# Two-layer decoder trunk on one core: other tiles for the turned first features, and another spacing of the first slabs

## The chip, the core and the metric

The kernel runs on one core of a Trainium2 chip. A core has a matmul engine (TensorE, PE in the profile; its weight loads are shown as PEld), VectorE (DVE), ScalarE (ACT), GpSimd (POOL) and SyncE (SP), which issues most of the transfers from memory. The engines run side by side, each through its own list of instructions, and wait for one another by semaphores. The metric is the time of one execution on the device in microseconds (us). The time before is the median of 3 runs.

## The reference

What is computed, cut to the part that the change touches, is a trunk of two layers over 256 tokens of width 2048. Each layer has a mixing part (pooling and memory attention in the first, differential and memory attention in the second) and a feed-forward part:

```
D_MODEL, SEQ, D_FF = 2048, 256, 8192

def squared_relu_mlp(h, w1, w2):
    z = jax.nn.relu(h @ w1)
    return (z * z) @ w2

for i in range(2):
    ...
    x = x + jnp.concatenate([token_out, mem_out], axis=-1) @ w_out[i]
    x = x + squared_relu_mlp(rms_norm(x, ffn_norm[i]), w_ff1[i], w_ff2[i])
```

All weights and activations are 32-bit floats. The change touches the feed-forward part alone, and so acts twice, once in each layer.

## The kernel before

**Precision.** Each weight and each activation is split into a high half (a rounded copy, made on ACT at L187) and a low half (what is left, made on DVE at L190). A product takes high by high, low by high and high by low. The halves of the weights stand in two rings of 6 slots, hi_ring and lo_ring; the class Feed loads the weights (DMAs from SP at L151 to L155, into buffers named raw, slab and room, and accumulating DMAs from POOL at L162) and splits them up to 3 jobs ahead of PE.

**Features and tiles.** The 8192 hidden features are 64 columns of 128, numbered by when they are made. The first 8 come out of first_jobs: a product with fewer multiplications (seven where eight would be plain, in the manner of Strassen) over the first 1024 columns of w_ff1, in seven accumulators p0 to p6 that hold seven banks of PSUM. The other 56 come out of up_tile, one at a time, tiles 0 to 55. A tile is 16 blocks of 128 x 128 weights; a block is one matmul of 512 columns (L448) and one of 256 (L450). All tiles from 2 on accumulate in the one PSUM bank left, named x_bank. After a tile, ACT copies the bank out (evict, L809), and only then can PE start in it again. Some steps later the feature is squared and split into z, and for each pair of features the four sums that the cheap product needs are made (combine, into sit).

**Slabs.** The second product, z by w_ff2, uses the cheap scheme as well for half of the rows and columns that it covers. It is cut into slabs; a slab is a pair of features by 1024 columns, four jobs (0 to 3) with two, one, two and two products of three matmuls each (product, L922, L924, L925; 21 matmuls of 512 columns in all). The seven accumulators serve two halves g = 0 and 1 of the output columns in turn; between them, swap copies the partial sums out and in again (L1080, L1072). The eight slabs numbered -8 to -1 are those of first_jobs. When the last of them ends, close_first puts the seven accumulators together (copies on ACT, adds on DVE, L1011).

**The turn.** The results of first_jobs stand with tokens on the partitions, and z wants features there. So turn_first, called four times (h = 0 to 3), transposes two features each on PE (L1044) through x_bank, evicts them (L809) and puts them through the same squaring (L1048, L1053) and splitting (L820, L824) as the tiles. The tuple turned_at names the tiles ahead of which this happens. It also sets the numbering: the list feat gives each turned pair the next two numbers, so that the tiles behind it get numbers higher by two, and slabs take the features by their numbers.

**The order of the work.** tiles_at(p) says at which tile the slab p is to begin. From it a list of jobs is made, each with a due time in tiles: job 0 of slab p+1, jobs 1 and 2 of slab p and job 3 of slab p-1 share a place. While the tiles are written out, due(u) runs all jobs that are due, at every fourth block of a tile, and at least two jobs ahead of a tile and one behind a turn if they are ready. A job isn't ready while its accumulators belong to the other half, or while the features (z) or the sums (sit) of its slab aren't made. A job that isn't ready holds up all jobs behind it. Twelve jobs are left for the end, between the tiles of the last product. The framework's scheduler may then shift instructions on an engine, within what data and buffers allow.

```
        turned_at = (18, 26, 34, 42)
...
        for u in range(2, 56):
            due(u, 2)
            if u in turned_at:
                turn_first(turned_at.index(u))
                due(u, 1)
...
            up_tile(index[u], bank(), inner(u))
```

Of the kernel before, what the change touches and what calls it, by code (L numbers as in the profile page):

```python
# [303 lines left out]
def program(ctx, tc, plan, dry, xT, memT, par, lam, cst, wst, yT):  # L304
# [468 lines left out]
    def ffn(l, xs, tags, done, z, sums_in, f_place):  # L773
# [20 lines left out]
        z_done, sit_done, summed_up = set(), set(), set()  # L794
        z_free = {j: j < 8 for j in range(NK)}
        sit_free = [False] * 4
        turned_at = (18, 26, 34, 42)
        feat, index = [], []
        for u in range(56):
            if u in turned_at:  # L800
# [378 lines left out]
        def tiles_at(p):  # L1179

            if p <= 0:
                return 9.08 + 0.86 * p
            return 9.08 + 0.78 * p if p <= 47 else 45.74 + 1.6 * (p - 47)

        jobs = []
        for p in range(-9, len(slabs) + 1):
            for j, s in enumerate((p + 1, p, p, p - 1)):
                if -8 <= s < len(slabs):
                    when_due = tiles_at(p) + j * (tiles_at(p + 1) - tiles_at(p)) / 4
                    jobs.append((when_due, s, j))  # L1190
# [321 lines left out]

    x_in = []
    down = ffn(0, fx, ("S1", "S0"), lambda n: resid_done(n, [(x_in[0], G_KV)], False), *made)
    x_kv = sp.tile([P, NK, 512], F32R, tag="S2", name="x_kv")
    x_in.append(x_kv)
# [237 lines left out]
    made = out_tiles(1, cat1, lead1, [15, 11], fx1, flush, (0, 1, 3, 7, 10), "S2")  # L1754

    down = ffn(1, fx1, ("S2", "S1"), lambda n: nc.sync.dma_start(yT[:, n, :], resid[:, n, :]), *made)
    down()
    flush()
# [82 lines left out]
```

## Time and profile before

| what | us |
|---|---|
| median of 3 runs | 2001.18 |
| lowest and highest of them | 1998.41, 2003.38 |
| the profiled execution | 2000.19 |
| its span, first to last instruction | 1998.4 |
| PE busy | 1989.0 |
| DVE busy | 1769.7 |
| ACT busy | 1547.3 |

The profiled execution is the one that all views show. Its span is 1.8 us shorter than its time. The feed-forward part of layer 0 stands roughly between 260 and 920 us of the span, that of layer 1 between 1330 and 1990 us. A row of a timeline gives the start in us, the length, the engine, the line, the operation with output and input, and in brackets the idle time before it and what ended it. Matmuls are pipelined: the length of one (0.39 us for 512 columns) is longer than the distance to the next start, and the distance is what counts for the time. In the windows, the numbers behind the stretch are its length, the busy time of PE, PEld, DVE, ACT and POOL with their instruction counts, the clock that was granted to TensorE (1.00 is full), the share of the DMA engines, and GB/s.

### The profile page before, as it was taken

Reading aid. Unit: us, or ns where it says so; the run is one execution under the profiler, and the core shown is the slowest. Engines: PE = TensorE matmul, PEld = TensorE weight load, DVE = VectorE, ACT = ScalarE, POOL = GpSimd, SP = SyncE. Lnnn points to the kernel's source line nnn. Section 1 sums busy time; section 2 is a strip of 40 time slices with the busy share of each in tenths; the row PEclk is TensorE's granted clock in tenths of the full one; section 3 lists DMA queues with packets and bytes.
Section 4 is the critical chain, followed back from the end, with each engine's and each line's share of the span. In section 5 each row is a group of like instructions: output and inputs, shape, how many; then the busy total and the mean of one; then the engine's idle time right before and its main releaser. Section 6 shows DMA issues by size and latency. Waiting matters only on the chain.

```text
span 1998.4 us, 31885 instructions
## 1 busy us (share of the span) xinstructions
PE 1989.0 (100%) x10386; PEld 1691.0 (85%) x10386; DVE 1769.7 (89%) x3252; ACT 1547.3 (77%) x2858; POOL 221.5 (11%) x261
## 2 busy tenths in 40 slices
PE   9999999999999999999999999999999999999999
PEld 7888888888888888888888889888888888888888
DVE  8888889999999999889765698989999999999988
ACT  7766677788888878778665699777778888878775
POOL 0000011111111211100000000001111112111110
PEclk9999999999999999999999999999999999999999
DMA  9556578988888888765565534568888888887775
GB/s 318 175 191 192 190 203 217 248 223 244 232 236 229 229 218 236 212 192 187 185 235 192 169 127 143 191 197 232 235 223 241 226 241 234 229 248 194 221 211 145
DMA packets 147623, 424.29 MB, mean 212 GB/s; under 512 B 16640, under 2 KB 19328, under 8 KB 147456
## 3 DMA queue, kind: packets, MB, share of 16 engines
q1 hardware_dynamic: 110448, 355.12, 53.0%
q0 software_dynamic: 36864, 67.13, 20.4%
q8 instruction: 81, 1.33, 0.3%
q14 instruction: 86, 0.70, 0.1%
q10 hardware_dynamic: 144, 0.01, 0.0%
HBM read 420.10 MB, written 2.10 MB: 211 GB/s over the span
## 4 chain that ended last, share of the span: by engine, by line
PE 98%; DMA 1%; DVE 0%; ACT 0%; issue 0%; SPq 0%; ACTq 0%
PE x_bank L448 22%; PE x_bank L450 11%; PE p L925 10%; PE p L922 10%; PE p L924 10%; PE wo L448 6%; PE wo L450 3%; PE u L448 2%; PE ff L448 1%; PE u L450 1%; PE q L482 1%; PE q L484 1%; PE k L482 1%; PE q L483 1%; PE v L482 1%; PE k L483 1%
## 5 line engine op out<-in xcount | busy, mean ns | idle before, releaser
L187 ACT CAST hi_ring<-raw 128x512 fp32r<-128x512 f32 x937 | 572.8, 620 | 229.0 <-DVE lo_ring L190 59.6
L190 DVE TENSOR_TENSOR lo_ring<-raw,hi_ring 128x512 fp32r<-128x512 f32 x937 | 633.6, 688 | 106.5 <-ACT hi_ring L187 92.4
L448 PE MATMUL x_bank<-fx,hi_ring 128*128 128x512 f32 x1728 | 542.4, 395 | 1.6 <-ACT room L809 1.6
L450 PEld LDWEIGHTS x_bank<-fx,lo_ring 128*128 128x128 f32 x1728 | 325.2, 188 | 74.7 <-DVE lo_ring L190 1.0
L190 DVE TENSOR_TENSOR lo_ring<-room,hi_ring 128x1024 fp32r<-128x1024 f32 x256 | 312.7, 1223 | 47.2 <-ACT hi_ring L187 44.5
L187 ACT CAST hi_ring<-room 128x1024 fp32r<-128x1024 f32 x256 | 268.8, 1053 | 97.0 <-PE x_bank L448 50.1
L450 PE MATMUL x_bank<-fx,lo_ring 128*128 128x256 f32 x1728 | 340.6, 279 | 0.1
L448 PEld LDWEIGHTS x_bank<-fx,hi_ring 128*128 128x128 f32 x1728 | 287.0, 189 | 28.8 <-ACT room L809 3.9
L190 DVE TENSOR_TENSOR lo_ring<-slab,hi_ring 128x1024 fp32r<-128x1024 f32 (+1 forms) x256 | 244.3, 954 | 28.2 <-ACT hi_ring L187 25.1
L187 ACT CAST hi_ring<-slab 128x1024 fp32r<-128x1024 f32 (+1 forms) x256 | 211.8, 835 | 50.0 <-PE p L924 23.1
L162 POOL DMA_DIRECT2D slab<-in_w x128 | 110.6, 864 | 1256.1 <-DVE lo_ring L190 1244.0
L922 PE MATMUL p<-hi_ring,sit 128*128 128x512 f32 x480 | 188.5, 393 | 0.0
L924 PE MATMUL p<-hi_ring,sit 128*128 128x512 f32 x480 | 187.5, 391 | 0.0
L925 PE MATMUL p<-lo_ring,sit 128*128 128x512 f32 x480 | 186.0, 390 | 0.0
L162 POOL DMA_DIRECT2D room<-in_w x128 | 110.5, 863 | 487.3 <-DVE lo_ring L190 421.9
L448 PE MATMUL wo<-cat,hi_ring 128*128 128x512 f32 x512 | 161.6, 397 | 0.0
L922 PE MATMUL p<-hi_ring,z 128*128 128x512 f32 x368 | 144.9, 394 | 0.0
L925 PE MATMUL p<-lo_ring,z 128*128 128x512 f32 x368 | 143.7, 391 | 0.3 <-DVE lo_ring L190 0.3
L924 PE MATMUL p<-hi_ring,z 128*128 128x512 f32 x368 | 143.9, 391 | 0.0
L450 PEld LDWEIGHTS wo<-cat,lo_ring 128*128 128x128 f32 x512 | 95.9, 188 | 22.3
L925 PEld LDWEIGHTS p<-lo_ring,sit 128*128 128x128 f32 x480 | 89.9, 188 | 20.6 <-DVE lo_ring L190 1.4
L922 PEld LDWEIGHTS p<-hi_ring,sit 128*128 128x128 f32 x480 | 90.0, 188 | 14.1 <-ACT p L1072 0.6
(415 smaller groups left out, 3522.1 us busy)
## 6 DMA issues: line engine op xcount, KB each, us to landing
raw<-in_w SPq DMA_DIRECT2D x466, 512.0 KB, 4.2
slab<-in_w SPq DMA_DIRECT2D x128, 512.0 KB, 5.7
room<-in_w SPq DMA_DIRECT2D x128, 256.0 KB, 4.7
slab<-in_w POOLq DMA_DIRECT2D x128, 256.0 KB, 5.1
room<-in_w POOLq DMA_DIRECT2D x128, 256.0 KB, 5.6
memraw<-in_mem SPq DMA_DIRECT2D x5, 512.0 KB, 3.6
resid<-in_x SPq DMA_DIRECT2D x8, 256.0 KB, 5.3
out_y<-resid SPq DMA_DIRECT2D x16, 128.0 KB, 1.9
```

The lines of the kernel that those rows point to most:

```text
L162: self.nc.gpsimd.dma_start(t, self.wst[h, :, 0:512], accum_op=ALU.add)
L187: self.last_cast = self.nc.scalar.copy(hi, src)
L190: low = self.nc.vector.tensor_sub(lo, src, hi.bitcast(F32))
L448: nc.tensor.matmul(ps, hi, xs[:, k, :], start=first and c == 0, stop=False)
L450: nc.tensor.matmul(ps[:, T : 2 * T], lo, xs[:, k, 0:T], start=False, stop=last and c == len(ks) - 1,)
L482: nc.tensor.matmul(ps[t], x[t][1], hi, start=k == 0, stop=False)
L483: nc.tensor.matmul(ps[t], x[t][0], hi, start=False, stop=False)
L484: nc.tensor.matmul(ps[t], x[t][0], lo, start=False, stop=k == NK - 1)
L922: nc.tensor.matmul(ps, a[1], hi, start=new, stop=False, **again)
L924: nc.tensor.matmul(ps, a[0], hi, start=False, stop=False, **again)
L925: nc.tensor.matmul(ps, a[0], lo, start=False, stop=end, **again)
```

## The change

Two tables of numbers in ffn are changed. The turns stand ahead of tiles 16, 24, 32 and 38. The first eight slabs begin 0.8 tile apart, from 8.5 back, the slabs 0 to 4 one tile apart from 8.5 on, and from slab 4 on the distance of 0.78 stays, counted from 12.5; behind slab 47 it is 1.6 as before.

```
-        turned_at = (18, 26, 34, 42)
+        turned_at = (16, 24, 32, 38)
...
             if p <= 0:
-                return 9.08 + 0.86 * p
-            return 9.08 + 0.78 * p if p <= 47 else 45.74 + 1.6 * (p - 47)
+                return 8.5 + 0.8 * p
+            if p <= 4:
+                return 8.5 + p
+            return 12.5 + 0.78 * (p - 4) if p <= 47 else 46.04 + 1.6 * (p - 47)
```

Both programs have the same 10,273 matmuls; their order differs. Two places show how.

The first is on PE, at the fourth turn of layer 0. The names are p_ for the seven accumulators with z or sit, and x_bank with fx for the tiles. In the kernel before:

```order
L925 MATMUL p_2841<-lo_ring,sit_1884 128x512
L448 MATMUL x_bank<-fx_1723,hi_ring 128x512 x2
L450 MATMUL x_bank<-fx_1723,lo_ring 128x256 x2
L448 MATMUL x_bank<-fx_1723,hi_ring 128x512 x2
L450 MATMUL x_bank<-fx_1723,lo_ring 128x256 x2
L1044 MATMUL x_bank<-const,f_d 128x128
L1044 MATMUL x_bank<-const,room_2682 128x128
L1044 MATMUL x_bank<-const,f_d 128x128
L1044 MATMUL x_bank<-const,room_2682 128x128
L448 MATMUL x_bank<-fx_1723,hi_ring 128x512 x2
L450 MATMUL x_bank<-fx_1723,lo_ring 128x256 x2
```

Tile 41 ends, the transposes follow at once, and tile 42 follows them at once. In the changed kernel, at the same turn (now between tiles 37 and 38):

```order
L925 MATMUL p_2841<-lo_ring,sit_1884 128x512
L1044 MATMUL x_bank<-const,f_d 128x128
L1044 MATMUL x_bank<-const,room_2682 128x128
L1044 MATMUL x_bank<-const,f_d 128x128
L1044 MATMUL x_bank<-const,room_2682 128x128
L922 MATMUL p_2757<-hi_ring,z_1883 128x512
L924 MATMUL p_2757<-hi_ring,z_1883 128x512
L925 MATMUL p_2757<-lo_ring,z_1883 128x512
L922 MATMUL p_2758<-hi_ring,z_1883 128x512
L924 MATMUL p_2758<-hi_ring,z_1883 128x512
L925 MATMUL p_2758<-lo_ring,z_1883 128x512
L448 MATMUL x_bank<-fx_1723,hi_ring 128x512 x2
```

Slab matmuls now stand on both sides of the transposes; the first row is the last of twelve ahead of them.

The second place is on DVE, where the first slabs are closed in layer 0 (L1011 are the adds of close_first, L190 the low halves of weights that PE waits for). In the kernel before:

```order
L1011 TENSOR_TENSOR f_u<-f_u,p_2839 128x256
L190 TENSOR_TENSOR lo_ring<-room_2682,hi_ring 128x1024
L1011 TENSOR_TENSOR f_u<-f_u,p_2839 128x256
L190 TENSOR_TENSOR lo_ring<-slab_3401,hi_ring 128x1024
L1011 TENSOR_TENSOR f_d<-room_2682,f_u 128x256 x2
L1011 TENSOR_TENSOR f_d<-f_d,p_2840 128x256 x2
L190 TENSOR_TENSOR lo_ring<-raw_3359,hi_ring 128x512
```

And in the changed kernel:

```order
L190 TENSOR_TENSOR lo_ring<-room_2682,hi_ring 128x1024
L866 TENSOR_TENSOR room_2682<-room_2682 128x256
L190 TENSOR_TENSOR lo_ring<-slab_3376,hi_ring 128x1024
L1011 TENSOR_TENSOR f_u<-f_u,p_2839 128x256 x2
L1011 TENSOR_TENSOR f_d<-room_2682,f_u 128x256 x2
L1011 TENSOR_TENSOR f_d<-f_d,p_2840 128x256 x2
L190 TENSOR_TENSOR lo_ring<-raw_3331,hi_ring 128x512
```

The six adds of the third closing step stand in a row, behind the two wide low halves that parted them before.

## The prediction

> **What bounds the kernel now.** I read the page first, then the waits in total, then the windows of the two feed-forward stages, and last the timeline of TensorE (PE) at the few places where it stood still.
>
> ```profile
> span 1998.4 us, 31885 instructions
> PE 1989.0 (100%) x10386; PEld 1691.0 (85%) x10386; DVE 1769.7 (89%) x3252; ACT 1547.3 (77%) x2858; POOL 221.5 (11%) x261
> ```
>
> PE is busy for 1989.0 of 1998.4 us, so the kernel is bound by the number of matmuls and by nothing else for most of its length. Both kernels issue the same matmuls in another order; an order can only win back time in which PE waits or runs slowly. All of that together is small, so the question is where in the two feed-forward layers it lies. The list of waits (waiter, line, what it waited for, us in total, times, longest) has two rows of PE that are longer than all its others:
>
> ```profile
> PE x_bank L1044 <- ACT room L809: 2.8, 2, 2.2
> PE x_bank L448 <- ACT room L809: 1.6, 2, 0.8
> ```
>
> L1044 is the transpose in turn_first. It waits only 2 times, once in each layer, although it is called four times in each. Both times it waits for the copy at L809 that empties the one bank called x_bank. The timeline shows the two places; the first is layer 0, the second layer 1 (start, us, engine, line, operation, idle before it):
>
> ```profile
> 727.59 0.39 PE L450 MATMUL x_bank<-fx,lo_ring 128*128 128x256 f32 x2
> 728.66 0.33 PE L1044 MATMUL x_bank<-const,f_d 128*128 128x128 f32 x1 [0.68 <-ACT room L809]
> ...
> 729.04 0.27 PE L1044 MATMUL x_bank<-const,room 128*128 128x128 f32 x1
> 730.03 0.73 PE L448 MATMUL x_bank<-fx,hi_ring 128*128 128x512 f32 x2 [0.72 <-ACT room L809]
> ```
>
> ```profile
> 1795.34 0.39 PE L450 MATMUL x_bank<-fx,lo_ring 128*128 128x256 f32 x2
> 1797.88 0.33 PE L1044 MATMUL x_bank<-const,f_d 128*128 128x128 f32 x1 [2.15 <-ACT room L809]
> ...
> 1798.27 0.27 PE L1044 MATMUL x_bank<-const,room 128*128 128x128 f32 x1
> 1799.38 0.93 PE L448 MATMUL x_bank<-fx,hi_ring 128*128 128x512 f32 x2 [0.84 <-ACT room L809]
> ...
> 1803.09 0.66 PE L448 MATMUL x_bank<-fx,hi_ring 128*128 128x512 f32 x2
> ```
>
> This is the fourth turn, ahead of tile 42. In this kernel no p matmul stands between tile 41, the transposes and tile 42, so PE sits through the emptying of x_bank twice. A turn with p work around it costs nothing, as the second turn of layer 0 shows:
>
> ```profile
> 539.24 0.39 PE L450 MATMUL x_bank<-fx,lo_ring 128*128 128x256 f32 x2
> 539.47 0.40 PE L922 MATMUL p<-hi_ring,sit 128*128 128x512 f32 x1
> ...
> 540.62 0.40 PE L925 MATMUL p<-lo_ring,sit 128*128 128x512 f32 x1
> 540.85 0.27 PE L1044 MATMUL x_bank<-const,f_c 128*128 128x128 f32 x1
> ...
> 541.18 0.27 PE L1044 MATMUL x_bank<-const,f_u 128*128 128x128 f32 x1
> 541.21 0.48 PE L922 MATMUL p<-hi_ring,z 128*128 128x512 f32 x1
> ```
>
> There six p matmuls (539.47 to 540.85, 1.38 us, so 0.23 us each) hide the copy before the transposes, and the transposes follow without idle time. That row is my measure of cover: 1.38 us is enough.
>
> **The change, term by term.** My sum is made against the profiled execution's own time, 2000.19 us (span 1998.4); the median of the runs shown is 2001.18, which is 1.0 above it.
>
> *The fourth turn moves from tile 42 to 38.* The order of the changed kernel puts 12 p matmuls ahead of the transposes (12 x 0.23 = 2.8 us) and six behind them (1.4 us), against none and none. The cause of the hole was readiness: slab 43 starts with features 46 and 47, which tiles 40 and 41 made just in time to be late; with the turn at 38, they come out of tiles 38 and 39. What goes, from the rows above:
> - Layer 0, before the transposes: two 256-column matmuls from 727.59 take 0.23 us (539.24 to 539.47 is such a pair), so the transposes could start at 727.82; they start at 728.66: 0.84 us.
> - Layer 0, behind them: the last starts at 729.04 and takes 0.11 us of PE (540.85 to 541.18 is three of them), so PE is free at 729.15; the tile starts at 730.03: 0.88 us.
> - Layer 1, in the same way: 1797.88 - 1795.57 = 2.31 us, and 1799.38 - 1798.38 = 1.00 us.
> - Layer 1, slow matmuls: from 1799.38 to 1803.09 run three groups of two blocks, 3.71 us. Such a group is two 512-column matmuls of 0.23 us and a pair of 0.23, so 0.7 us, and 3.71 - 2.1 = 1.6 us are too much.
>
> The sum is 0.84 + 0.88 + 2.31 + 1.00 + 1.6 = 6.6 us. The slow stretch goes only if the hole made it. The windows bear on that (PE, PEld, DVE, ACT and POOL busy, then the granted clock and the DMA share):
>
> ```profile
> 727.00:730.00 3.00, 1.64 (x11) 1.11 (x9) 1.19 (x3) 1.85 (x5) 0.00 (x0) 1.00 1.04 419
> 1795.00:1799.00 4.00, 1.39 (x9) 0.86 (x7) 1.03 (x2) 1.67 (x4) 0.00 (x0) 1.00 0.80 321
> 1799.00:1803.00 4.00, 3.62 (x12) 3.10 (x13) 2.50 (x9) 3.36 (x8) 0.00 (x0) 0.59 0.03 10
> ```
>
> The granted clock is 1.00 through both holes and falls to 0.59 right behind the longer one. In layer 0 ordinary matmuls pause for 2.2 us (727.82 to 730.03) and no dip follows; in layer 1 for 3.8 us (1795.57 to 1799.38), and it does. I take the 1.6 us as part of the hole; if the dip had another cause it would stay, which is a rival below. The Trainium skill, page "TensorE: Matmul & The Clock Gate", section "What's actually happening", says that the clock is halved after an idle window of some 3.4 us and comes back after a busy one as long; its section "Part 4: PE-mode transpose" adds that transposes do not count as busy in the same way. By that rule the dip belongs to the hole, and the trace's 3.8 and 2.2 us lie on its two sides; by the other reading the sum would lose 1.6.
>
> *The crowd behind the turn goes too.* In this kernel the waiting slab jobs run all at once after tile 42. The change has no such crowd: its longest stretch of p work is 12 matmuls. These rows show what the crowd costs PE:
>
> ```profile
> 739.82 0.39 PE L924 MATMUL p<-hi_ring,sit 128*128 128x512 f32 x1
> 740.13 0.49 PE L925 MATMUL p<-lo_ring,z 128*128 128x512 f32 x1
> 740.47 0.39 PE L925 MATMUL p<-lo_ring,sit 128*128 128x512 f32 x1
> ```
>
> 0.31 and 0.34 us in place of 0.23 are 0.2 us; with the same in layer 1, 0.4 us.
>
> *The first slabs: 0.8 tile apart, then 1.0.* A tile is worth some 6 us of PE and a slab's 21 matmuls 4.8 us (0.23 each), so a first slab with its share of tile goes from 0.86 x 6 + 4.8 = 10.0 us to 9.6 us. Everything moves forward by 0.58 tile at the start of the second kind of slab and falls back to 0.3 tile late from slab 4 on; no work is added. VectorE (DVE) is the engine that could suffer, since it makes a low half for every block and also closes the first products (L1011) at tiles 7 to 9. It loses a little there now:
>
> ```profile
> 262.00:324.00 62.00, 62.00 (x321) 52.85 (x320) 56.10 (x93) 46.67 (x80) 11.21 (x13) 1.00 0.82 222
> 324.00:345.00 21.00, 20.49 (x101) 16.29 (x100) 18.83 (x32) 14.12 (x23) 3.45 (x4) 1.00 0.76 195
> 1396.00:1417.00 21.00, 20.95 (x104) 17.00 (x103) 19.61 (x34) 15.87 (x26) 3.45 (x4) 1.00 0.73 201
> ```
>
> PE loses 0.5 us of idle time in layer 0 (21.00 - 20.49) and 0.05 in layer 1 at the closing; as each such stop also delays the next starts, I count 1.2 us for both as the most that the change can win here. What it can cost: in the changed order the six adds of closing step 2 stand in a row, where two wide low halves parted them. The four of this kernel that stand together take 1.34 us (341.64 to 342.98 below); six take 2.0, so DVE brings no low half for 0.7 us longer, 1.3 us over both layers if all of that reaches PE.
>
> ```profile
> 341.64 0.76 DVE L1011 TENSOR_TENSOR f_d<-room,f_u 128x256 f32<-128x256 f32 x2
> 342.31 0.75 DVE L1011 TENSOR_TENSOR f_d<-f_d,p 128x256 f32<-128x256 f32 x2
> 342.98 1.29 DVE L190 TENSOR_TENSOR lo_ring<-raw,hi_ring 128x512 fp32r<-128x512 f32 x2
> ```
>
> Against it, slabs 1.0 apart give DVE more room just behind. I take 0 between -1.2 and +1.3.
>
> *The other three turns* (16, 24, 32 for 18, 26, 34) keep cover: 9, 12 and 12 p matmuls ahead, 6, 6 and 4 behind; 9, 6 and 12 and 6, 5 and 4 stand there now, without a wait. The exchange of the banks' partial sums (copies on ScalarE, ACT) now falls beside tile 20, whose bank change has only six p matmuls of cover, and beside turns 2 to 4. Nothing shows its cost; it lies between 0 (the 1.38 us above sufficed) and one copy of 0.6 us late at each of three places in two layers, 3.6 us. I take 0.3, near the row that sufficed.
>
> Sum: 2000.19 - 6.6 - 0.4 + 0 + 0.3 = **1993.5 us**.
>
> **The rivals.** *Loads are late in any case* (DMA as the next bound). What speaks for it: the longer hole began with a late load.
>
> ```profile
> 1796.72 0.62 ACT L187 CAST hi_ring<-raw 128x512 fp32r<-128x512 f32 x1 [2.62 <-DMA raw<-in_w]
> raw<-in_w SPq DMA_DIRECT2D x466, 512.0 KB, 4.2
> 1789.11 7.54 DMA raw<-in_w
> ```
>
> A load that takes 4.2 us at the median took 7.54. Against it: in the order before, eight groups of tile matmuls run with no slab between them, so tile weights are called for faster than anywhere else; in the change no stretch of tile matmuls is longer there than elsewhere in the middle of the stage. If the lateness stayed, layer 1 would keep what its hole has over layer 0's, 2.31 - 0.84 = 1.5 us, perhaps in both layers: 1993.5 + 3.0 = 1996.5 us.
>
> *The dip of the clock has another cause*: 1993.5 + 1.6 = 1995.1 us.
>
> *The wait only moves*, to the bank changes beside the copies of the exchange: the upper end of that term, 1993.5 + 3.3 = 1996.8 us.
>
> *Slower*: DVE becomes the bound in tiles 2 to 9. In the 62 us before the closing it is busy for 56.10, so it has 5.9 us of room. Slabs 0.8 instead of 0.86 tile apart raise its work per us of PE by 4% at most (10.0 / 9.6), 2.3 us, which fits. It would decide only from about 10% on; at 22%, an extra 7 us in each layer, the time would be 1993.5 + 14 = 2007.5 us.
>
> *The change does not do what it says*, because the scheduler puts the transposes bare again: the order shows that it does not, so this has no chance of its own.
>
> **How the numbers follow.** Forecast 0.62; late loads 0.13; another cause of the dip 0.05; moved wait 0.17; slower 0.03. The low end takes the whole win at the closing and no cost of the copies, with 2 us for what the order may smooth beyond the rows that I counted: 1993.5 - 1.2 - 0.3 - 2.0 = 1990. The high end takes in the two rivals of 1996.5 and 1996.8 with the 1.3 of the closing: 1998. A measurement of this kernel tells about 0.3% (6 us) from no change, so against 2001.18 faster means below 1995.2. The forecast lies only 1.7 us inside that. I give 0.53 of the forecast's 0.62 to that side, and 0.07 of the three rivals between 1995 and 1997: faster 0.60, within 0.3% 0.37, slower 0.03.
>
> **What would show it right or wrong.** Right: no idle time before L1044 in either layer, no row with a clock under 1.00 in the middle of layer 1, and 4.4 us less of PE's idle time (0.68 + 0.72 + 2.15 + 0.84). The closing is judged by PE's waits for lo_ring near tiles 7 to 9, the copies by waits at bank changes near tile 20 and the turns. The prediction is wrong if holes of the same size stand elsewhere, above all behind a late load, or if the runs before owe their time to something outside these two layers.

## The result, and the profile after

| kernel | median, us | lowest to highest | runs | profiled span, us |
|---|---|---|---|---|
| before | 2000.08 | 1998.41 to 2003.38 | 4 | 1998.4 |
| changed | 1990.30 | 1989.81 to 1991.01 | 4 | 1987.7 |

The ratio is 0.9949, with a 95% interval of 0.9932 to 0.9967: the change is faster by 0.5%, outside the 0.3% within which this kernel's runs tell nothing. The profiled execution of the changed kernel took 1989.81 us, 10.4 less than that of before.

The page of the changed kernel has these first lines, to be held against the two of before:

```profile
span 1987.7 us, 31886 instructions
PE 1982.7 (100%) x10386; PEld 1690.8 (85%) x10386; DVE 1766.7 (89%) x3252; ACT 1545.9 (78%) x2858; POOL 221.5 (11%) x261
```

The profile counts the same 10386 matmuls in both kernels (the 10,273 named ahead of the prediction is not this count), and PE is busy 6.3 us less although it does the same work. The span has fallen by 10.7 us. So 6.3 of these stood in the profile as busy time: matmuls whose recorded length covers a late start, or which ran at a lower clock. The list of PE's waits in total (waiter, line, what it waited for, us, times, longest) has become short:

```profile
PE mk L475 <- ACT hi_ring L187: 0.8, 1, 0.8
PE warm L388 <- PEq L1816: 0.8, 1, 0.8
```

Both stand ahead of the two feed-forward parts. No wait for x_bank is left. The timeline of PE shows why at the fourth turn of layer 0, now ahead of tile 38:

```profile
676.99 0.39 PE L450 MATMUL x_bank<-fx,lo_ring 128*128 128x256 f32 x2
677.22 0.40 PE L922 MATMUL p<-hi_ring,sit 128*128 128x512 f32 x1
...
679.78 0.39 PE L925 MATMUL p<-lo_ring,sit 128*128 128x512 f32 x1
680.01 0.27 PE L1044 MATMUL x_bank<-const,f_d 128*128 128x128 f32 x1
...
680.36 0.47 PE L922 MATMUL p<-hi_ring,z 128*128 128x512 f32 x1
...
681.60 0.40 PE L925 MATMUL p<-lo_ring,z 128*128 128x512 f32 x1
681.83 0.39 PE L448 MATMUL x_bank<-fx,hi_ring 128*128 128x512 f32 x1
```

Twelve p matmuls (677.22 to 680.01, 2.8 us) stand ahead of the transposes and six behind them, and nothing has an idle time in brackets. Layer 1 is the same, with the transposes at 1744.16. The windows around it have full clock, where before had 0.59 right behind the hole:

```profile
1740.00:1748.00 8.00, 8.00 (x43) 6.64 (x42) 7.96 (x13) 7.45 (x13) 1.73 (x2) 1.00 0.68 197
1748.00:1752.00 4.00, 4.00 (x23) 3.41 (x22) 3.12 (x7) 4.00 (x9) 0.86 (x1) 1.00 0.89 216
```

Because much of the loss does not stand as idle time, I made a ledger from the timelines. For each pair of neighbouring matmuls it takes the distance between their starts, less the distance that such a pair has where nothing is late (0.23 us behind one of 512 columns, 0.115 behind one of 256). What is over is PE's loss, in us, summed by tiles for layer 0 / layer 1. A cell moves by some 0.1 us with the distance that is taken as not late.

| tiles | before | changed | won, both layers |
|---|---|---|---|
| 6 to 10, the closing | 1.53 / 0.66 | 0 / 0 | 2.2 |
| 11 to 15 | 0 / 0 | 0.08 / 0.08 | -0.2 |
| 16 to 19 | 0.44 / 0.44 | 0.01 / 0.01 | 0.9 |
| 20 to 37 | 0.48 / 0.37 | 0.51 / 0.54 | -0.2 |
| 38 to 41, with the fourth turn of before | 1.82 / 3.41 | 0 / 0 | 5.2 |
| 42 to 44 | 0.81 / 2.31 | 0.11 / 0.25 | 2.8 |
| 45 to 55 | 0.63 / 0.69 | 0.63 / 0.65 | 0 |

It adds up to 10.7 us, which is the whole difference of the spans. So the time came from two places: the fourth turn with what stands behind it (8.0) and the closing of the first products (2.2), for which the prediction had written 0.

### The profile page after: what moved, and what is told of

It is laid out like the page before. It is cut to its first block, busy times and chain, and to the rows that moved or that the text cites. A ratio compares the mean times of both kernels' runs of the same rounds, so it can differ in the third digit from the quotient of the medians.

```text
span 1987.7 us, 31886 instructions
## 1 busy us (share of the span) xinstructions
PE 1982.7 (100%) x10386; PEld 1690.8 (85%) x10386; DVE 1766.7 (89%) x3252; ACT 1545.9 (78%) x2858; POOL 221.5 (11%) x261
## 4 chain that ended last, share of the span: by engine, by line
PE 99%; DMA 0%; SPq 0%; ACT 0%; issue 0%; DVE 0%
PE x_bank L448 22%; PE x_bank L450 11%; PE p L922 10%; PE p L924 10%; PE p L925 10%; PE wo L448 6%; PE wo L450 3%; PE u L448 2%; PE ff L448 1%; PE u L450 1%; PE q L482 1%; PE k L482 1%; PE q L484 1%; PE q L483 1%; PE v L482 1%; PE k L483 1%
## 5 line engine op out<-in xcount | busy, mean ns | idle before, releaser
L190 DVE TENSOR_TENSOR lo_ring<-raw,hi_ring 128x512 fp32r<-128x512 f32 x937 | 632.6, 686 | 101.2 <-ACT hi_ring L187 89.0
L190 DVE TENSOR_TENSOR lo_ring<-room,hi_ring 128x1024 fp32r<-128x1024 f32 x256 | 312.5, 1222 | 43.2 <-ACT hi_ring L187 41.6
L190 DVE TENSOR_TENSOR lo_ring<-slab,hi_ring 128x1024 fp32r<-128x1024 f32 (+1 forms) x256 | 244.0, 953 | 32.2 <-ACT hi_ring L187 29.4
```

The lines of the kernel that those rows point to most:

```text
L190: low = self.nc.vector.tensor_sub(lo, src, hi.bitcast(F32))
```

## The experiments

All ratios are against runs of the kernel before on the same chip; its medians there were between 1998.87 and 1999.81 us. What an expectation calls a theory is written out in it.

### Each half of the change alone

turns_only has the new turned_at with the old spacing; spacing_only has the new spacing with the old turned_at; fourth_only moves the fourth turn alone:

```
turned_at = (16, 24, 32, 38)   # turns_only, with the old tiles_at
turned_at = (18, 26, 34, 42)   # spacing_only, with the new tiles_at
turned_at = (18, 26, 34, 38)   # fourth_only, with the old tiles_at
```

> Only the four turns move (16, 24, 32, 38); the spacing of the slabs is that of the kernel before. Theory A (three separate sums, read from the starts of PE: 8.0 us at the fourth turn, 2.2 us at the closing of the first slabs in tiles 6 to 10, 0.9 us in tiles 16 to 19): the hole at the fourth turn and the 0.9 us go, the closing still loses about 2.2 us over both layers, so some 8 to 9 us below the profiled execution of before, near 1991.5 to 1992.5 us. Rival B (the spacing does nothing by itself, the closing was only late because a load was late): as fast as the changed kernel, 1990.3 us, and no wait for lo_ring in tiles 6 to 10. Rival C (the win is mostly the spacing): above 1995 us.

> Only the spacing of the slabs changes; the turns stay at 18, 26, 34 and 42. Its order puts six slab matmuls ahead of the transposes of the fourth turn and two behind them, where the kernel before has none. Theory A: the closing no longer loses its 2.2 us, the hole ahead of the transposes goes (six matmuls, 1.38 us, sufficed at another turn), the one behind them shrinks from 0.9 us to about 0.4 in each layer, and the dip of the clock goes with the hole: 1991 to 1993 us. Rival C (the hole hangs on the tile at which the turn stands, not on the cover): the hole stays, 1996 to 1998 us.

> The kernel before with the fourth turn alone moved from tile 42 to 38; the other turns and the spacing stay. Theory A: the hole of 8.0 us goes, the closing (2.2 us) and the loss in tiles 16 to 19 (0.9 us) stay: 1992 to 1993 us, about 1 us above the kernel with all four turns moved. Rival: the loss in tiles 16 to 19 is no matter of the first turn, and this is as fast as the kernel with all four turns moved.

> The kernel before once more, for a second trace. Theory A says that the hole before the transposes in layer 1 was 1.5 us longer than in layer 0 only because one load landed 7.5 us after its issue: the base of each hole is 0.84 us before and 0.9 us behind the transposes in both layers, the rest varies from run to run, and the clock dips only behind a hole that is longer than some 3 us in all. Rival: the lateness belongs to the order, and the hole of layer 1 is 2.3 us again, with the dip.

| kernel | median, us | lowest to highest | ratio | loss, tiles 6 to 10 | loss, tiles 38 to 41 |
|---|---|---|---|---|---|
| turns_only | 1993.55 | 1992.92 to 1994.12 | 0.9968 [0.9956, 0.9981] | 1.50 / 0.50 | 0 / 0 |
| spacing_only | 1992.12 | 1991.77 to 1992.34 | 0.9960 [0.9945, 0.9975] | 0 / 0 | 0.83 / 0.82 |
| fourth_only | 1994.08 | 1992.39 to 1994.50 | 0.9971 [0.9959, 0.9983] | 1.36 / 0.36 | 0 / 0 |
| before_again, one run | 1999.68 | | | 1.35 / 0.45 | 1.82 / 3.04 |

The median of before beside them is 1999.37. The halves win 5.8 and 7.2 us, the whole change 9 to 10: they overlap. turns_only and fourth_only are each over 1 us slower than was expected of them. In turns_only the moved turns also cost something: tiles 20 to 37 lose 1.2 us in each layer where the kernel before loses 0.4, and 0.55 of it stands behind the third turn, where a slab's matmul waits for its low half (614.83 and 1680.36). In fourth_only layer 1 loses 1.4 us at tiles 19 and 21 (1538.37 and 1552.13); why was not tried. Moving the fourth turn removes its hole; the new spacing nearly removes it too, for the slabs come to other tiles, and six p matmuls then stand ahead of the old turn. What is left there is another wait, in the list of PE's waits of spacing_only:

```profile
PE p L922 <- ACT hi_ring L187: 0.9, 2, 0.5
```

Only the new spacing takes away the loss at tiles 6 to 10. And in before_again the pause behind the fourth turn of layer 1 was 3.4 us, from the two 256-column matmuls (1796.83, 0.23 us long together) to the tile at 1800.49, and the clock stayed full:

```profile
1796.83 0.39 PE L450 MATMUL x_bank<-fx,lo_ring 128*128 128x256 f32 x2
...
1800.49 0.73 PE L448 MATMUL x_bank<-fx,hi_ring 128*128 128x512 f32 x2 [0.84 <-ACT room L809]
```

```profile
1800.00:1804.00 4.00, 3.51 (x20) 3.06 (x21) 3.04 (x9) 4.00 (x9) 0.00 (x0) 1.00 0.03 11
```

### Does the hole make the dip of the clock?

Two kernels lengthen the hole of the fourth turn: ACT repeats the copy that empties the bank of the four transposed blocks, which the output doesn't need.

```
+                for _ in range(2):      # 5 in hole_5
+                    nc.scalar.copy(x, t4.rearrange("p c t -> p (c t)"))
```

> The kernel before, with the fourth turn's copy out of the bank made three times instead of once, which lengthens the second half of the hole by about 2 x 0.5 us in each layer. The pause between ordinary matmuls was 2.2 us in layer 0 and 3.4 to 3.8 us in layer 1 so far, with a dip of the granted clock behind 3.8 and none behind 3.4 and 2.2. Theory D (the dip follows the length of the pause): about 3.2 us in layer 0 without a dip, 4.4 us or more in layer 1 with one. Rival (the dip has another cause): no dip, or one that stands elsewhere.

> As the last, with the copy made six times: about 2.5 us longer in each layer. Theory D: pauses of about 4.7 us in layer 0 and 6 us in layer 1, each with a dip behind it to half the clock, each dip costing about 1.6 us. Rival: layer 0 shows no dip.

One execution of each took 2006.68 and 2010.35 us. Layer 0, which has no dip in the kernel before, has one in both. For hole_2 that was not expected: its pause in layer 0 was to be 3.2 us, too short for a dip, and came out longer. These are hole_2's timeline and windows there:

```profile
727.82 0.39 PE L450 MATMUL x_bank<-fx,lo_ring 128*128 128x256 f32 x2
...
731.85 0.73 PE L448 MATMUL x_bank<-fx,hi_ring 128*128 128x512 f32 x2 [2.31 <-ACT room L1048]
...
732.75 1.05 PE L448 MATMUL x_bank<-fx,hi_ring 128*128 128x512 f32 x2
```

```profile
728.00:732.00 4.00, 1.02 (x7) 0.58 (x7) 1.66 (x6) 3.26 (x8) 0.00 (x0) 1.00 0.69 281
732.00:735.00 3.00, 3.00 (x11) 2.52 (x12) 1.76 (x6) 2.64 (x5) 0.00 (x0) 0.59 0.00 0
```

Ordinary matmuls pause from 728.05 to 731.85, 3.80 us, and the window behind has a mean granted clock of 0.59: it is 0.50 for 3.41 us, from 732.53 on. The clock stays full behind the pauses of 2.2 us (layer 0 of before and before_again) and of 3.43 us (layer 1 of before_again), and falls at those of 3.80 us here and 3.81 us in layer 1 of before. So the dip belongs to the hole: a longer hole makes one where none was.

How long a pause must be is less clear, for the clock can fall before the pause is over. In layer 1 of hole_2 ordinary matmuls pause from 1798.77 to 1804.32, and a window inside the pause has the dip already:

```profile
1800.00:1804.00 4.00, 1.12 (x4) 0.72 (x4) 1.92 (x6) 3.21 (x8) 0.00 (x0) 0.61 0.36 145
...
1804.32 1.22 PE L448 MATMUL x_bank<-fx,hi_ring 128*128 128x512 f32 x2 [2.26 <-ACT room L1048]
```

The trace's clock falls there at 1800.90, 2.1 us after the last ordinary matmul; in the other dips it falls 3.7 to 5.6 us after it (hole_5 731.90 and 1807.10, before 1799.73, hole_2 732.53). Each of these dips lasts 3.41 or 6.83 us at half the clock. So all pauses of 3.80 us and more here have a dip and none up to 3.43 us has, but the length alone does not say when the clock falls.

Nor does every execution of the kernel before have a dip. The record holds the mean granted clock of each: 1.000 in 51 of 67 later ones, with a median of 1998.9 us, and 0.998 or 0.999 in the other 16, with a median of 2001.4 us. A dip of 3.41 us at half clock takes 0.0009 off that mean. The profiled execution of before, with 0.999, is one of the minority. All kernels without the hole have 1.000 in every execution.

### Which step of the spacing removes the loss at tiles 6 to 10?

no_relief takes the four steps of 1.0 away from the changed kernel; slow_firsts sets the first eight slabs 0.86 apart again, and keeps the rest:

```
# no_relief
-            if p <= 4:
-                return 8.5 + p
-            return 12.5 + 0.78 * (p - 4) if p <= 47 else 46.04 + 1.6 * (p - 47)
+            return 8.5 + 0.78 * p if p <= 47 else 45.16 + 1.6 * (p - 47)
# slow_firsts
-                return 8.5 + 0.8 * p
+                return 8.5 + 0.86 * p
```

> The changed kernel without the four wide steps: first slabs 0.8 tile apart, all later ones 0.78 apart from 8.5 on. Theory A1 (the closing of the first slabs costs nothing in the changed kernel because the wide steps leave VectorE time right behind it): the loss in tiles 6 to 10 comes back, 1 to 3 us over both layers, and PE waits for lo_ring there; 1992 to 1994 us. Theory A2 (it costs nothing because the first slabs come earlier): no loss there, and the time is that of the changed kernel within 1 us, but for a turn or tile with little cover.

> The changed kernel with its first eight slabs 0.86 tile apart, as before, and the four wide steps kept. Theory A1: no loss in tiles 6 to 10, 1990 to 1991 us. Theory A2: the loss of 1.8 to 2.2 us comes back, about 1992.3 us.

no_relief took 1995.02 us (1994.42 to 1996.12, ratio 0.9979 [0.9969, 0.9989]) and lost 0.14 / 0.19 in tiles 6 to 10; what it takes over the changed kernel stands elsewhere: 0.8 in each layer at the first turn, which has only two p matmuls behind it there, 1.1 in each behind tile 50, and the rest in pieces. slow_firsts took 1993.33 (1992.81 to 1994.41, ratio 0.9969 [0.9957, 0.9981]) and lost nothing in tiles 6 to 10, but 0.90 / 1.15 in tiles 2 to 5. So neither theory held: no_relief was to lose 1 to 3 us at the closing or to stay within 1 us of the changed kernel, and slow_firsts was to take 1990 to 1991 us or to lose its time in tiles 6 to 10. Neither step by itself is what the closing wants. The loss had moved in slow_firsts, together with a wait of ACT that the timeline shows:

```profile
293.48 0.62 ACT L187 CAST hi_ring<-raw 128x512 fp32r<-128x512 f32 x1 [1.78 <-DMA raw<-in_w]
```

The kernel before has such a wait at tile 8. Its timeline, with the load that ACT waits for (SPq) and the step that frees that load's buffer (DVE at 328.07, done at 328.76):

```profile
328.07 0.69 DVE L190 TENSOR_TENSOR lo_ring<-raw,hi_ring 128x512 fp32r<-128x512 f32 x1
...
328.79 4.88 SPq L151 DMA_DIRECT2D raw<-in_w  x2
...
331.88 0.40 ACT L820 CAST z<-stage 128x256 fp32r<-128x256 f32 x1
...
334.24 0.62 ACT L187 CAST hi_ring<-raw 128x512 fp32r<-128x512 f32 x1 [1.96 <-DMA raw<-in_w]
334.76 1.04 ACT L187 CAST hi_ring<-room 128x1024 fp32r<-128x1024 f32 x1
...
334.89 0.69 DVE L190 TENSOR_TENSOR lo_ring<-raw,hi_ring 128x512 fp32r<-128x512 f32 x1 [1.03 <-ACT hi_ring L187]
...
337.12 0.50 PE L925 MATMUL p<-lo_ring,z 128*128 128x512 f32 x1 [0.29 <-DVE lo_ring L190]
```

ACT stands for 1.96 us, DVE then for 1.03, and everything behind comes later until PE waits for a low half at 337.12. The adds of the closing are not what is waited for first.

### Do the raw loads stand behind slab loads?

My first reason for the late load was SP's list: raw loads stand in it behind slab loads that wait for buffers. slab_pool_b (in the kernel before) and slab_pool_a (in the changed one) issue the loads at L153 from GpSimd, slab_both_b and slab_both_a those at L155 too; PE's order is the same.

```
-                self.nc.sync.dma_start(t, self.wst[h])
+                self.nc.gpsimd.dma_start(t, self.wst[h])
# slab_both also:
-                self.nc.sync.dma_start(t[:, 512:1024], self.wst[h, :, 512:1024])
+                self.nc.gpsimd.dma_start(t[:, 512:1024], self.wst[h, :, 512:1024])
```

> Theory E (in the kernel before, the raw load that ScalarE waits for at tile 8 is late because it stands behind a slab load in SyncE's list, which itself waits 5.4 us for its buffer): with the slab loads issued by GpSimd, ScalarE no longer waits 1 to 2 us for raw at tile 8 in either layer, the loss of PE in tiles 6 to 10 (1.4 and 0.6 us) is under 0.3 us in each layer, the late load ahead of the fourth turn in layer 1 (2.3 to 2.6 us) is under 0.5 us, so that layer 1's hole is about as long as layer 0's (0.84 us before the transposes instead of 1.9 to 2.3), and the time is 2.5 to 4 us under that of the kernel before, 1995 to 1997 us. Rival (the load is late for another reason, such as the DMA engines' own rate or the buffers of raw): the wait at tile 8 and the loss stay within 0.5 us of what they are, the time is 1998.5 to 2000.5 us. Third reading (GpSimd issues more slowly or stands behind its own work): slab loads land late, and PE waits at slabs instead; over 2002 us.

> After the run with only the first half of the slab loads on GpSimd, ScalarE still waited 2.0 and 2.4 us for raw at tile 8, and SyncE still issued nothing from 321.9 to 328.6 us of the profile: the second loads of a slab (L155) then waited for their buffer in its list instead. Theory E2 (the raw load stands behind whichever slab load waits for a buffer): with both kinds on GpSimd, the raw load goes out as soon as its own buffer is free, ScalarE's wait for raw at tile 8 is under 0.5 us in both layers, PE loses under 0.3 us in tiles 6 to 10 of each layer (1.5 and 0.7 in the kernel before), and the time is 1995.5 to 1998 us if no slab load gets late instead. Rival F (the load waits for its own buffer or for the DMA engines): the wait stays at 1 to 2.4 us and the loss at 0.5 to 2 us, 1999 to 2001 us. Third reading (slab loads stand behind each other on GpSimd and land late): the raw wait goes but PE loses more than 0.5 us at slab matmuls, 1998 us or more.

> Theory E: in the changed kernel the same edit has only the wait for raw at tile 5 of layer 0 (1.8 us) to remove, which costs PE nothing, so the time stays within 1 us of the changed kernel's 1990.3. Rival (raw loads are late all through the stage behind slab loads, and ScalarE runs closer than PE's waits show): 2 us less or more. Third reading (GpSimd issues more slowly): over 1992 us.

> Theory E2: in the changed kernel the wait for raw at tile 5 of layer 0 (1.81 us) goes; PE has no loss there to win, so the time is 1989.5 to 1991 us. Rival F: the wait stays between 1.5 and 3.1 us, with up to 1.1 us of PE's time (as the run with half of the slab loads on GpSimd lost in tiles 2 to 5 behind a wait of 3.03 us). Third reading (slab loads late): over 1991.5 us.

| kernel | median, us | lowest to highest | ratio | ACT's wait at the early cast | PE's loss, same place |
|---|---|---|---|---|---|
| slab_pool_b | 2001.09 | 1999.27 to 2003.95 | 1.0009 [0.9999, 1.0018] | 1.99 / 2.37 | 1.54 / 1.95 |
| slab_both_b | 2000.73 | 1999.72 to 2003.89 | 1.0009 [0.9999, 1.0018] | 1.67 / 1.71 | 1.25 / 1.27 |
| slab_pool_a | 1990.38 | 1990.29 to 1991.25 | 0.9958 [0.9941, 0.9974] | 3.03 / none | 1.12 / 0 |
| slab_both_a | 1990.51 | 1989.99 to 1990.77 | 0.9954 [0.9939, 0.9968] | 2.56 / none | 0.65 / 0 |

The theory fell. In slab_both_b only raw loads are left in SP's list there, and the load at tile 8 is still late:

```profile
329.30 4.88 SPq L151 DMA_DIRECT2D raw<-in_w  x2
...
334.46 0.62 ACT L187 CAST hi_ring<-raw 128x512 fp32r<-128x512 f32 x1 [1.67 <-DMA raw<-in_w]
```

It goes out when its own buffer is free, and lands 5.1 us later. (In slab_both_a the view puts the wait of 2.56 us down to PE; the load landed at 303.51 and the cast began at 303.59.) One thing did go: the late load at tile 41 that made the hole of layer 1 longer than that of layer 0. Both kernels have 1.82 us in tiles 38 to 41 of each layer. So there the place of the slab loads mattered; whether by SP's list or by the load on the transfers wasn't tried apart. The medians didn't fall with it: slab_pool_b lost 1.3 us more at the early cast of layer 1, and slab_both_b 0.8 us more there than before_again, and 1.3 more in tiles 42 to 49 of that layer. The profiled execution of slab_pool_b is also the fastest of its ten, so what the others lost stands in no trace.

### The cast that stands out of turn

The order of ACT's casts of raw weights gives the answer. Raw loads are numbered as PE needs them, each holds two casts, and there are four buffers. At tile 8 of layer 0 the casts stand like this:

```
before:      117 117 123 119 119 121 121 123
one_turn_b:  117 117 119 119 121 121 123 123
```

The first half of raw123 stands four casts ahead of its turn. Its load can go out only when raw115 (four loads back) is done with, at 328.76, so it lands at 334.2; the data of raw119 and raw121, on chip since 324.2 and 326.2, wait behind it, since ACT works through its list in order. Layer 1 has the same at raw507. one_turn_b moves these two casts, and nothing else directly, back to their turn, by an order between instructions that is no wait on the chip; PE's order changes with it in 62 places, all behind the two closings (from 354 and from 1421 us on):

```
+    def in_turn(self, feed, job, cast):
+        if job[0] == "N":
+            if feed.last_n is not None and self.row["N", job[1] // 2] in (123, 507):
+                feed.order(cast, feed.last_n.ins.name)
+            feed.last_n = cast
+        return cast
...
-        self.last_cast = self.nc.scalar.copy(hi, src)
+        self.last_cast = self.plan.in_turn(self, job, self.nc.scalar.copy(hi, src))
```

in_turn_a does so for all such casts of the changed kernel (without the condition on 123 and 507), and PE's order stays word for word the same.

> The runs with slab loads on GpSimd left the wait for raw at tile 8 as it was (2.0 and 1.7 us in layer 0, 2.4 and 1.7 in layer 1), so the load does not stand behind slab loads. Theory G: in ScalarE's list of the kernel before, the cast that waits (first half of raw123 in layer 0, raw507 in layer 1) stands four casts ahead of its turn, in front of raw119 and raw121 that landed 8 to 10 us before; its own load goes out 0.03 us after DVE frees the buffer of raw115 and lands 5.4 us later. Here only these two casts are ordered behind the cast that precedes them in turn; the loads' order is unchanged. Expected: no wait of ScalarE for raw over 0.5 us at tile 8, PE's loss in tiles 6 to 10 (1.5 and 0.7 us) under 0.3 us in each layer, the holes at the fourth turn unchanged, and 1.5 to 2.5 us less than the kernel before, 1997 to 1998.5 us. Rival A (DVE's adds of the closing cause the loss): the wait for raw goes but PE still loses over 0.8 us in tiles 6 to 10 of layer 0, and the time stays within 1 us of the kernel before.

> All tile casts of the changed kernel in turn, PE's order unchanged. Theory G: the only early cast that waited there was raw111's at tile 5 of layer 0 (1.81 us), which cost PE nothing, so 1989.5 to 1991 us, the same as the changed kernel. Rival: casts in turn keep slots of the ring busy longer and a cast gets late elsewhere, over 1991.5 us.

> The changed kernel once more, on the same chip as the two others: 1990 to 1991 us, no wait at any of the four turns, no loss in tiles 6 to 10, a wait of ScalarE for raw of about 1.8 us at tile 5 of layer 0 and none over 0.5 us at tile 8. If the closing's win was one execution's luck, a loss of 0.5 to 1.5 us stands there.

one_turn_b took 1997.31 us (1995.01 to 1999.65, ratio 0.9990 [0.9981, 0.9999]) against 1999.54. ACT's timeline at the same place:

```profile
331.56 0.61 ACT L187 CAST hi_ring<-raw 128x512 fp32r<-128x512 f32 x1
332.07 0.40 ACT L820 CAST z<-stage 128x256 fp32r<-128x256 f32 x1
332.90 1.06 ACT L187 CAST hi_ring<-room 128x1024 fp32r<-128x1024 f32 x1 [0.43 <-PE p L924]
334.29 0.62 ACT L187 CAST hi_ring<-raw 128x512 fp32r<-128x512 f32 x1 [0.32 <-PE x_bank L448]
```

No cast waits for a load, and PE's loss in tiles 6 to 10 is 0.04 / 0.03 where it was 1.53 / 0.66. That is 2.1 us in the profile. The closing's adds are all still there. The medians differ by 2.2 us, but their interval reaches from 0.2 to 3.8 us, and the fourth turn's hole was to stay as it was and did not: it is 2.55 / 2.62, where before had 1.82 / 3.41 and before_again 1.82 / 3.04, since ACT now waits 1.8 us for a load ahead of it in both layers, and the profiled execution has no dip. So that the medians come so near is in part luck; the ledger and the missing wait carry the proof.

In all nine executions of kernels with the old spacing, the waits and losses keep one relation:

| execution | wait at the early cast | loss in tiles 6 to 10 |
|---|---|---|
| before | 1.96 / 1.08 | 1.53 / 0.66 |
| before_again | 1.78 / 0.86 | 1.35 / 0.45 |
| turns_only | 1.93 / 0.87 | 1.50 / 0.50 |
| fourth_only | 1.79 / 0.78 | 1.36 / 0.36 |
| hole_2 | 2.04 / 0.83 | 1.61 / 0.38 |
| hole_5 | 2.12 / 0.77 | 1.70 / 0.33 |
| slab_pool_b | 1.99 / 2.37 | 1.54 / 1.95 |
| slab_both_b | 1.67 / 1.71 | 1.25 / 1.27 |
| one_turn_b | none | 0.04 / 0.03 |

The loss is the wait less 0.37 to 0.45 us in all sixteen cases that wait: 0.4 us of cover, and beyond it each tenth of lateness reaches PE. In the changed kernel another cast is four early, raw111's at tile 5 of layer 0:

```profile
302.70 0.62 ACT L187 CAST hi_ring<-raw 128x512 fp32r<-128x512 f32 x1 [1.81 <-DMA raw<-in_w]
```

It waits 1.81 us and costs PE 0.02; in spacing_only it waits 1.96 us and costs 0.05. The longer waits of slab_pool_a and slab_both_a at the same cast (3.03 and 2.56) cost 1.12 and 0.65, so the cover there is 1.9 us. That is the difference that the new spacing makes: in layer 0 the early cast falls on a place with more cover, and in layer 1 of the changed kernel no cast waits for a load there.

after_again took 1990.56 us (1990.07 to 1991.16, ratio 0.9955 [0.9940, 0.9970]), with no loss in tiles 6 to 10 and no wait at a turn, like the changed kernel's first runs. in_turn_a took **1989.44** (1989.37 to 1989.77, ratio 0.9950 [0.9933, 0.9966]), the fastest kernel here, some 1 us under the changed one in runs that do not overlap with it. My expectation was 1989.5 to 1991. In the ledger of the feed-forward parts the two are alike to 0.1 us a layer, and the two profiled spans are 1987.6 and 1987.7 us, so where that last microsecond comes from is not settled.

### More cover at the turns

more_cover asks for two due jobs behind each turn instead of one, in the changed kernel:

```
                 turn_first(turned_at.index(u))
-                due(u, 1)
+                due(u, 2)
```

The same is done behind turn_left.

> Both theories of the bare turn expect little: the four turns of the changed kernel wait for nothing (6 to 12 p matmuls stand on both sides), so another due job ahead of and behind each turn has no wait left to remove. 1989.8 to 1991 us if cover is all that counts there; up to 1 us less if the 0.44 and 0.47 us that tiles 28 to 37 lose, and the 0.7 us of tiles 45 to 49, are bank changes with too little cover; over 1992 us if tiles elsewhere are left with only three to six p matmuls of cover and wait.

1992.17 us (1991.86 to 1992.56, ratio 0.9965 [0.9952, 0.9978]): slower than the changed kernel by about 1.8. The turns have nothing to win, and PE loses 1.13 us in each layer behind tile 50 that it didn't lose before: at 855.67 and 1920.97 a slab's first matmul waits for its high half. Its list of waits has the row:

```profile
PE p L922 <- ACT hi_ring L187: 1.8, 2, 0.9
```

## Why the prediction was right or wrong

The forecast was 1993.5 us for an execution that took 1989.81. The direction, and the fourth turn as the main reason, were right. The win was 6.7 us by the sum and 10.4 by the executions; the missing 3.7 to 4 us lie in the small terms. The sign that the prediction gave for the turn came true to the tenth: PE's idle time fell from 9.4 to 5.0 us, by 4.4. What it missed stood mostly as busy time. By its steps:

- **The fourth turn, 6.6 us: right.** The ledger has 1.82 for layer 0 and 3.41 for layer 1, and 1.6 of slow matmuls behind it, 6.8 in all. The order's twelve and six p matmuls hide both copies. But the 6.6 is that of one execution: in before_again the hole was worth 4.9, since the late load was shorter and there was no dip, and only 16 of 67 later executions of before show a lower clock. That the sum was made on one of these is chance. turns_only and fourth_only show the hole's going by itself.
- **The dip as part of the hole: right, and shown** by hole_2 and hole_5, which make a dip in layer 0. The rival of another cause falls. How long a pause must be is not settled, since in hole_2 the clock fell 2.1 us into one.
- **The crowd behind the turn, 0.4: too small.** Tiles 42 to 44 lost 0.81 in layer 0 and 0.7 in layer 1 beside the dip, and lose 0.11 and 0.25 now, so 1.1 were to be had.
- **The closing, "I take 0 between -1.2 and +1.3": this is the step that failed.** It named DVE's adds in a row as the risk and the reason, and counted 1.2 us as the most that could be won. The changed kernel has the six adds in a row and loses nothing; the loss was that of a cast ahead of its turn, which waits for its load, and it was worth 2.2 us, beyond the 1.2 that the term allowed. The row that the prediction quoted (PE idle for 0.5 us in 21) hid it: 0.3 us stood as idle time at 337.12 while the start was 0.46 us late, and the rest stood as busy time. A ledger of start distances shows 1.53 in layer 0 from the trace of before alone.
- **The copies of the exchange and the other turns, +0.3: wrong in sign for the change as a whole.** Tiles 11 to 37 lose 0.5 us less together than before. With the old spacing the moved turns do cost there, some 1.7 us in turns_only, so that the term stayed small hangs on the new spacing. What was won is 0.44 in each layer at tiles 16 to 19. Both halves alone leave part of it there (0.23 / 0.23 in turns_only, 0.33 / 0.31 in spacing_only). What made it was not tried.
- **The rivals.** Late loads did not stay: ACT has no wait over 0.7 us for raw behind tile 5 in either layer of the changed kernel. The wait did not move, as no wait of PE is left in the two feed-forward parts. DVE did not become the bound.
- **The range, 1990 to 1998,** holds the median of 1990.3, at its very low end. The sum was made for a profiled execution, and the one of the changed kernel took 1989.81 us, just below it. That the median still lies inside is luck: the 2 us "for what the order may smooth" happened to cover what the failed step owed.
- **Two sums were loose**, without weight for the forecast: a tile is 16 x 0.345 = 5.5 us of PE rather than 6, and the slow rival's 22% of DVE's 56.1 us is 6.4 us beyond its room, rather than 7.

What stays open: why the order of ACT's list puts one cast four places ahead (it is fixed before the program runs, and no run here shows by what rule), the loss at tiles 16 to 19, when in a pause the clock falls, and the last microsecond of in_turn_a.

## What to carry to other kernels

Where an engine's idle time is nearly zero, look for loss in the distances between starts: at the closing of layer 0 the idle time showed 0.5 us of 1.5. When a wait for a load appears, compare the order of the instructions that use the loads with the order in which the loads' buffers come free; one consumer ahead of its turn holds up everything behind it, and a change that seems to be about something else may only move it to a place with more cover. A single bank that is emptied and filled again wants matmuls on other banks on both sides of its copy.

## What the runs showed of the hardware

- A pause of ordinary matmuls can bring a dip of the clock, and four transposes inside the pause do not prevent it. No dip came with pauses of 2.2, 2.95, 3.02 (both in one_turn_b) and 3.43 us; the clock fell to 0.50 at pauses of 3.80 and 3.81 us and at the three longer ones of hole_2 and hole_5, for 3.41 or 6.83 us, and the dip cost 1.6 us in layer 1 of the kernel before. The Trainium skill, page "TensorE: Matmul & The Clock Gate", section "What's actually happening", gives an idle window of some 3.4 us. The lengths of the dips and the pauses behind which the clock fell agree with it; that it fell 2.1 us into one pause of hole_2 shows that a pause need not have lasted 3.4 us when the clock falls.
- Kernels that keep the hole have uneven times: the runs of before spread over 4.5 to 8 us beside each set of kernels, those of slab_pool_b, slab_both_b and one_turn_b over 4.2 to 4.7, those of all timed kernels without a hole of a microsecond over 0.4 to 2.1. The dip accounts for a part of it, 2001.4 against 1998.9 us at the median; but slab_both_b spreads over 4.2 us with a mean clock of 1.000 in all ten, so something else varies too, and what was not tried.
- A raw load of 512 KB landed 4.2 us after its issue at the median, and 5.4 us at tile 8 of layer 0, where a slab load and two others had gone out within 2.3 us before it. Taking the slab loads off SP's queue did not bring it down: 5.5 us there in slab_pool_b and 5.1 in slab_both_b, and 6.2 and 5.5 at the same place of layer 1, where it was 4.9.
